# A hybrid encoder layer as one stream of matmuls: weight loads on GpSimd's queue, and three more output units in the seven-product form

## The chip, the core and the metric

The kernel runs on one core of a Trainium2 chip. A core has five engines that run side by side, each with an instruction queue of its own that is worked off strictly in order: TensorE (PE in the profile; PEld is its loading of weights), VectorE (DVE), ScalarE (ACT), GpSimd (POOL) and SyncE (SP). PE multiplies into PSUM banks; DVE and ACT read those banks and work on tiles in SBUF; SP and POOL issue the DMAs that move tiles between SBUF and DRAM. An instruction waits in its queue for semaphores of others, and all that stand behind it wait too. The metric is the device time of one execution in microseconds (us), the median of three runs.

## The reference

One layer of a streaming encoder for 1024 positions of width 1024, in float32, cut to what matters here:

```python
h = rms_norm(x, norm1_w)
q, k, v, g_ret, x_lru, y_lru, gate_ret, gate_lru = split(h @ w_in)
o = head_group_norm(chunkwise_retention(rotary(q), rotary(k), v), ret_gn_w)   # 4 heads
y_a = (o * silu(g_ret)) @ w_ret_o
hl = rg_lru(causal_depthwise_conv(x_lru))                                     # 4 blocks
y_b = (hl * gelu(y_lru)) @ w_lru_o
x = x + (sigmoid(gate_ret + b0) * y_a + sigmoid(gate_lru + b1) * y_b) @ w_out
h = rms_norm(x, norm2_w)
gate, val = split(h @ ffn_w_up)                                               # 3072 each
x = x + (gelu(causal_depthwise_conv(gate)) * val) @ ffn_w_down
return rms_norm(x, norm_f_w)
```

## The kernel before

**Products in two parts.** Each float32 operand is split into a high part in the PE's reduced float32 type and a low part, the rest (`split`: a cast on ACT, L167, and a subtraction on DVE, L168). A product of two operands takes three matmuls (`PASSES`: high x high, high x low, low x high).

**Jobs.** The large projections are cut into jobs (`Job`). A job is one unit of 256 output columns, with operand blocks B11, B12, B21, B22 (the activations: first index the half of the inner dimension, second the half of the positions) and weight blocks A11 to A22. There are 28 jobs for the input projection, 4 for the retention output (`w_ro`, operand `og`), 4 for the LRU output (`w_lo`, operand `u`), then the output projection written out by hand (L1182), 24 jobs for the up projection and 12 for the down projection.

- The *standard form* (`mm_std`, matmuls at L330) takes 8 block products of 12 matmuls, 96 in all.
- The *seven-product form* (`mm_fast`, matmuls at L387; `fast=True`) is a Strassen-like scheme with 7 block products, 84 matmuls. It needs sums of weight blocks (S1 to S4, DVE at L246, L249, L255, L262), sums of operand blocks (T1 to T4, one set for all jobs of the operand; made by `tsets` for later operands) and more evictions from PSUM (ACT copies at L402, DVE additions at L413).

`FAST_RO` and `FAST_LO` say how many of the four jobs of each output projection take the seven-product form: 0 and 3. The order of the input jobs is the string `SEQ`: `g` a merge-gate job, `y` and `x` the two LRU jobs of a block, `h` the three jobs of a retention head.

**Queues in the program.** `loads()` brings raw weight blocks from DRAM, in the order of the jobs and at most `AHEAD` = 6 ahead, with `SY.dma_start` at L208; `preps()` splits and sums them (up to `NBLK` = 7 ready). `builders` make the operand of the coming projection while the current one runs; `back` holds generators of work that follows a job (a head's retention, an LRU block, rotary tables), which are advanced a little after each product. Operands, temporaries and results share 81 buffers `u` of 128x512; weights share 22 buffers `w`. The order on each engine is chosen by the framework's scheduler from the program's order and from priorities (`hp()`).

**What is kept in DRAM between stages.** `ret_out` writes the gated retention output of each head to `og_d` (L964); a `builder` started by `og_start`, after the last input job but one, reads it back (L997) and splits it into the 32 tiles of `og`. The LRU blocks write `u_d` (L853), and `u_start`, after the third retention output job, first drains all `back` work and then starts the builder of `u`, which also makes its T sums from `u_d` (L544 to L552). LRU gate matmuls are at L814. The up projection's results go through `post_ff` (conv, gelu, product at L1219) to `ff_d` by a DMA of GpSimd (L1220); the down projection reads `ff_d` as its weight blocks (L208) and `w_dn` (L1230) as its operand, and accumulates through `x1_d` (L1260, L1274). The rotary tables use eight more DMAs of GpSimd (L741 to L744). Every other DMA is issued by SP.

Of the kernel before, what the change touches and what calls it, by code (L numbers as in the profile page):

```python
# [11 lines left out]
F32 = mybir.dt.float32  # L12
# [5 lines left out]
P = 128  # L18
D = 1024
T = 1024  # L20
KT = 8
TH = 512
# [64 lines left out]
class Units:  # L87
# [11 lines left out]
    def get(self, dt=F32):  # L99
        i = self.q.popleft()  # L100
        self.count += 1
        t = self.pool.tile(self.shape, dt, tag=f"{self.name}{i}", name=f"{self.name}{i}_{self.count}")
        self.at[id(t)] = (i, t)
        return t

    def put(self, *tiles):
        for t in tiles:
            self.q.append(self.at.pop(id(t))[0])
# [8 lines left out]
RATE = 1.0  # L117
BRATE = 3.0
RESERVE = 20
FAST_RO = 0  # L120
RO_T = 9
FAST_LO = 3
GQ = False
SEQ = "g g y0 g y1 h0 h1 h2 h3 x0 g g x1 g y2 g x2 g y3 x3"
STD_L = 2


# [1 line left out]
def tile_trunk_layer(ctx, tc, x, xt, positions, params, consts, normf, w_in, w_ro, w_lo,  # L129
                     w_out, w_up, w_dn, w_gate, out):  # L130
    nc = tc.nc
    V, S, G, PE, SY = nc.vector, nc.scalar, nc.gpsimd, nc.tensor, nc.sync
    ST = G if GQ else SY

    pool = ctx.enter_context(tc.tile_pool(name="sb", bufs=1))
    pps = ctx.enter_context(tc.tile_pool(name="ps", bufs=1, space=bass.MemoryType.PSUM))
    pdr = ctx.enter_context(tc.tile_pool(name="dr", bufs=1, space=bass.MemoryType.DRAM))
# [6 lines left out]
    get, put = U.get, U.put  # L144
# [3 lines left out]
    ident = cst[:, C_ID:C_ID + P]  # L148

    og_d = pdr.tile([KT, P, T], F32, tag="og", name="og_d")  # L150
    u_d = pdr.tile([KT, P, T], F32, tag="u", name="u_d")
    y_d = pdr.tile([KT, P, T], F32, tag="y", name="y_d")
    sg_d = pdr.tile([2, KT, P, T], F32, tag="sg", name="sg_d")
# [10 lines left out]
    def split(src, get=get):  # L164

        hi, lo = get(F32R), get(F32R)
        S.copy(hi, src)  # L167
        V.tensor_sub(lo, src, hi.bitcast(F32))  # L168
        return hi, lo
# [29 lines left out]
    def loads():  # L199
        i = 0  # L200
        while True:
            while i >= len(queue):
                yield None
            jb = queue[i]
            for nm in jb.order:
                t = W.get()
                m, kh = int(nm[1]) - 1, int(nm[2]) - 1
                SY.dma_start(t, jb.src(m, kh))  # L208
                jb.raw[nm] = t
                state["raws"] += 1  # L210
                yield True
            i += 1
# [69 lines left out]
    builders = deque()  # L282
# [29 lines left out]
    def drain():  # L312
        while back:
            advance(1e9)
# [156 lines left out]
    def pair_src(w, i):  # L471
        return lambda m, kh: w[i, 2 * m + kh]
# [58 lines left out]
    def reads(fetch, keys, ahead):  # L531

        keys, got = deque(keys), deque()
        while keys or got:
            while keys and len(got) <= ahead:
                got.append(fetch(*keys.popleft()))
            yield got.popleft()

    def tsets(op, fetch, ahead=2):
        tiles = reads(fetch, [(n, j) for j in range(4) for n in ("B11", "B12", "B21", "B22")], ahead)  # L540
        for j in range(4):
            b11, b12, b21, b22 = (next(tiles) for _ in range(4))
            t1, t2 = get(), get()
            V.tensor_sub(t1, b12, b11)  # L544
            op["T1", j] = split(t1)
            yield 1.2
            V.tensor_sub(t2, b22, t1)
            op["T2", j] = split(t2)
            yield 1.2
            V.tensor_sub(b12, b12, b22)  # L550
            op["T3", j] = split(b12)
            V.tensor_sub(t2, b21, t2)  # L552
            op["T4", j] = split(t2)
            put(t1, t2, b11, b12, b21, b22)
            yield 2.4
# [11 lines left out]
    h1, keep = {}, {}  # L567
# [324 lines left out]
    def retention_head(hd, qk, vv):  # L892
        cur = 0
        mask = cst[:, C_MASK + 128 * hd:C_MASK + 128 * hd + 128]
        for h in range(2):
# [55 lines left out]
                yield 0.3  # L951
            put(kd[h], vt[h, 0], vt[h, 1], qk[0, h], qk[1, h])

    def ret_out(hd, gg):
        for h in range(2):
            for m in range(2):
                ps = psa.get()
                for b in range(4):
                    c0 = 256 * (b % 2) + 128 * m
                    PE.transpose(ps[:, 128 * b:128 * b + 128], ob[h, b // 2][:, c0:c0 + 128], ident)  # L960
                g = gg[m, h]
                V.scalar_tensor_tensor(g, ps, pc("ret_gn_w", 2 * hd + m), g, ALU.mult, ALU.mult)
                psa.put(ps)
                ST.dma_start(og_d[2 * hd + m, :, TH * h:TH * h + TH], g)  # L964
                put(g)
                yield 0.8
            put(ob[h, 0], ob[h, 1])
        if hd == HEADS - 1:
            put(*rot.values())
# [13 lines left out]
    def operand(op, fetch, sums=True):  # L983

        keys = [(n, j) for n in ("B11", "B21", "B12", "B22") for j in range(4)]
        for key, t in zip(keys, reads(fetch, keys, 3)):
            op[key] = split(t)
            put(t)
            yield 0.6
        if sums:  # L990
            yield from tsets(op, fetch)

    def from_dram(src):
        def fetch(n, j):
            t = get()
            h = int(n[2]) - 1
            SY.dma_start(t, src[4 * (int(n[1]) - 1) + j, :, TH * h:TH * h + TH])  # L997
            return t
        return fetch
# [18 lines left out]
    def emit_ret_o(n):  # L1018
        def emit(m, h, ps, unit):
            ch = 2 * n + m  # L1020
            t = ojobs[n].take(m, h)
            V.tensor_mul(t, ps, t)
            ST.dma_start(t1_d[ch, :, TH * h:TH * h + TH], t)
            put(t)
            if unit is not None:
                put(unit)
        return emit
# [48 lines left out]
    jobs[-1].last = True  # L1076
    def og_start(post=jobs[-2].post):
        builders.append(operand(og, from_dram(og_d), False))
        return post() if post else None

    jobs[-2].post = og_start

    def og_sums():
        drain()
        if FAST_RO:
            builders.append(tsets(og, from_dram(og_d)))

    def u_start():
        drain()
# [1 line left out]

    ojobs = []
    for n in range(4):
        ojobs.append(Job(pair_src(w_ro, n), og, emit_ret_o(n), {2: u_start, RO_T: og_sums}.get(n),
                        fast=n >= 4 - FAST_RO, last=n == 3, drop12=n == 3 - FAST_RO, fetch=from_sg(0, n)))
    for n in range(4):
        ojobs.append(Job(pair_src(w_lo, n), u, emit_lru_o(n), fast=n >= 4 - FAST_LO, last=n == 3,
# [109 lines left out]
    def post_ff(i):  # L1207
        g, kh, kk = i // 8, (i % 8) // 4, i % 4
        for h in range(2):
            c = get()  # L1210
            src = gv[0, h]
            S.activation(c, src, AF.Identity, bias=pc("ffn_conv_b", i), scale=pc("ffn_conv_w", 48 + i))  # L1212
            for s in (1, 2):
                w = pc("ffn_conv_w", 24 * (2 - s) + i)
                V.scalar_tensor_tensor(c[:, s:], src[:, :TH - s], w, c[:, s:], ALU.mult, ALU.add)  # L1215
                if h == 1:
                    V.scalar_tensor_tensor(c[:, :s], gv[0, 0][:, TH - s:], w, c[:, :s], ALU.mult, ALU.add)
            S.activation(c, c, AF.Gelu_apprx_tanh)
            V.tensor_mul(c, c, gv[1, h])  # L1219
            G.dma_start(ff_d[g, 4 * h:4 * h + 4, kh, :, kk, :].rearrange("t p c -> p t c"),  # L1220
                         c.rearrange("p (t c) -> p t c", t=4))
            put(c)
        for t in gv.values():
            put(t)
# [154 lines left out]
```

## Time and profile before

| | us |
|---|---|
| median of 3 runs | 1678.83 |
| lowest and highest run | 1673.21, 1679.45 |
| profiled execution, its own time | 1675.42 |
| its span, first to last instruction | 1673.6 |

| engine | busy us | share of the span |
|---|---|---|
| PE | 1627.2 | 97% |
| PEld | 1332.6 | 80% |
| DVE | 1289.9 | 77% |
| ACT | 886.4 | 53% |
| POOL | 40.7 | 2% |

A group's row of the profile reads: line, engine, operation, output <- inputs, shapes, count | busy us, mean ns of one | idle time of the engine before them, and what ended most of it. A row of the timeline reads: start, length, engine, line, operation, count, and in brackets the idle time before it and what ended it. "SPq" and "POOLq" are the queues in which DMAs are issued. A row of waits reads: engine and line <- what it waited for: us in total, times, longest.

### The profile page before, as it was taken

The page shows a single profiled execution, that of the slowest core. Times are in us where ns is not written, and L with a number is a line of the kernel's source. Part 1 is how long each engine was busy: PE and PEld are TensorE (multiplying, and loading weights), DVE is VectorE, ACT ScalarE, POOL GpSimd, SP SyncE. Part 2 cuts the span into 40 slices and gives each one's busy share as a digit, 9 for nine tenths or more (in the row PEclk, how much of TensorE's full clock was granted, in tenths as well). Part 3 has the DMA queues.
Part 4 walks back from the last instruction along what each step waited for, and adds up shares of the span by engine and source line. Part 5 has one row for each costly group of instructions (what it writes and reads, how often), then busy time and mean ns, then how long its engine had stood idle before and what let it go on. Part 6 is the DMA issues. An engine that isn't in the chain of part 4 may idle for free.

```text
span 1673.6 us, 21183 instructions
## 1 busy us (share of the span) xinstructions
PE 1627.2 (97%) x7224; PEld 1332.6 (80%) x7224; DVE 1289.9 (77%) x2366; ACT 886.4 (53%) x1480; POOL 40.7 (2%) x60
## 2 busy tenths in 40 slices
PE   8999999999999999999999999999999999999997
PEld 6888788888888877887778788888888887777776
DVE  8998768666888889857862796777767777878886
ACT  7654444535678877753530564444444455444554
POOL 0001000000000000000000000000000000000000
PEclk9999999999999999999999999999999999999999
DMA  7243212131333348656463022222222237687851
GB/s 293 89 154 97 86 54 89 51 95 45 113 114 105 122 140 267 210 166 232 154 209 107 32 95 82 82 82 82 89 82 82 92 122 229 224 260 243 260 193 76
DMA packets 120524, 225.97 MB, mean 135 GB/s; under 512 B 14048, under 2 KB 14176, under 8 KB 120416
## 3 DMA queue, kind: packets, MB, share of 16 engines
q1 hardware_dynamic: 116192, 210.99, 39.1%
q0 software_dynamic: 4224, 13.64, 2.1%
q8 instruction: 56, 0.92, 0.2%
q14 instruction: 52, 0.43, 0.1%
HBM read 164.80 MB, written 54.53 MB: 131 GB/s over the span
## 4 chain that ended last, share of the span: by engine, by line
PE 50%; DVE 8%; DMA 6%; ACT 3%; issue 2%; SPq 0%; DVEq 0%; ACTq 0%
PE g L387 36%; PE g L330 7%; PE g L1182 4%; DMA u<-w_dn 2%; DVE u L168 2%; PE a L814 2%; DVE w L168 1%; DMA w<-ff_d 1%; DMA x_d<-u 1%; DVE u L797 1%; ACT u L167 1%; DVE u L413 1%; DMA u<-u_d 1%; PE a L513 0%; DMA u<-w_out 0%
## 5 line engine op out<-in xcount | busy, mean ns | idle before, releaser
L387 PE MATMUL g<-u,w 128*128 128x512 f32 x5124 | 1204.7, 393 | 20.1 <-ACT u L402 9.7
L387 PEld LDWEIGHTS g<-u,w 128*128 128x128 f32 x5124 | 958.9, 188 | 224.6 <-ACT u L402 14.8
L167 ACT CAST w<-w 128x512 fp32r<-128x512 f32 x471 | 291.3, 621 | 359.7 <-PE g L387 280.6
L168 DVE TENSOR_TENSOR w<-w,w 128x512 fp32r<-128x512 f32 x471 | 322.6, 686 | 90.0 <-ACT w L167 85.4
L330 PE MATMUL g<-u,w 128*128 128x512 f32 x960 | 227.2, 394 | 2.8 <-ACT u L167 2.8
L167 ACT CAST u<-u 128x512 fp32r<-128x512 f32 x232 | 139.3, 620 | 150.1 <-DVE u L552 16.1
L330 PEld LDWEIGHTS g<-u,w 128*128 128x128 f32 x960 | 181.3, 190 | 41.9 <-ACT u L167 3.2
L168 DVE TENSOR_TENSOR u<-u,u 128x512 fp32r<-128x512 f32 x232 | 154.5, 687 | 38.8 <-ACT u L167 25.9
L413 DVE TENSOR_TENSOR u<-g,u 128x512 f32<-128x512 f32 x183 | 125.6, 686 | 57.0 <-PE g L387 43.5
L402 ACT COPY u<-g 128x512 f32<-128x512 f32 x183 | 106.4, 582 | 73.8 <-PE g L387 73.7
L1182 PE MATMUL g<-u,u 128*128 128x512 f32 x384 | 90.1, 392 | 2.5 <-ACT u L167 1.6
L1182 PEld LDWEIGHTS g<-u,u 128*128 128x128 f32 x384 | 71.3, 188 | 18.4 <-ACT u L167 2.0
L1215 DVE SCALAR_TENSOR_TENSOR u<-u,par,u 128x511 f32<-128x511 f32 (+1 forms) x96 | 71.6, 747 | 6.2 <-ACT u L1212 5.5
L1220 POOL DMA_DIRECT2D ff_d<-u x48 | 36.2, 753 | 1271.0 <-DVE u L1219 1271.0
L246 DVE TENSOR_TENSOR w<-w,w 128x512 f32<-128x512 f32 x61 | 42.1, 690 | 20.6 <-DMA w<-w_up 12.6
L814 PE MATMUL a<-u,u 128*128 128x512 f32 x192 | 48.8, 394 | 4.3 <-ACT u L167 3.5
L1184 DVE TENSOR_TENSOR u<-g,u 128x512 f32<-128x512 f32 x16 | 11.1, 691 | 49.3 <-PE g L1182 49.3
L1212 ACT ACTIVATE u<-u,par 128x512 f32<-128x512 f32 x48 | 39.1, 817 | 15.7 <-DVE u L413 15.7
L814 PEld LDWEIGHTS a<-u,u 128*128 128x128 f32 x192 | 35.5, 188 | 14.3 <-ACT u L167 5.6
L249 DVE TENSOR_TENSOR w<-w,w 128x512 f32<-128x512 f32 x61 | 42.0, 688 | 0.9
L262 DVE TENSOR_TENSOR w<-w,w 128x512 f32<-128x512 f32 x61 | 41.9, 686 | 0.4
L255 DVE TENSOR_TENSOR w<-w,w 128x512 f32<-128x512 f32 x61 | 41.8, 685 | 0.3
(173 smaller groups left out, 1151.2 us busy)
## 6 DMA issues: line engine op xcount, KB each, us to landing
w<-w_in SPq DMA_DIRECT2D x112, 256.0 KB, 2.7
w<-w_up SPq DMA_DIRECT2D x96, 256.0 KB, 2.6
u<-w_dn SPq DMA_DIRECT2D x96, 256.0 KB, 4.0
u<-x_d SPq DMA_DIRECT2D x56, 256.0 KB, 5.3
x_d<-u SPq DMA_DIRECT2D x48, 256.0 KB, 3.3
ff_d<-u POOLq DMA_DIRECT2D x48, 256.0 KB, 2.5
w<-ff_d SPq DMA_DIRECT2D x48, 256.0 KB, 3.8
u<-x SPq DMA_DIRECT2D x32, 256.0 KB, 5.3
```

The source lines that it names most:

```text
L167: S.copy(hi, src)
L168: V.tensor_sub(lo, src, hi.bitcast(F32))
L246: V.tensor_add(s1, a21, a22)
L249: V.tensor_sub(s1, s1, a11)
L262: V.tensor_sub(s1, a12, s1)
L330: PE.matmul(ps[h], w[a][:, c], o[b], start=n == 0, stop=n == 23)
L387: PE.matmul(bank, w[a][:, c], need(op, (bn, j))[b], start=first and n == 0, stop=n == 11, skip_group_check=True)
L402: S.copy(u, bank)
L413: V.tensor_add(u, bank, u)
L814: PE.matmul(ps, wg[g][a][:, cs], xs[k][b], start=q == 0, stop=q == 5)
L1182: PE.matmul(ps, o[a][:, 128 * t:128 * t + 128], wo[k][b], start=n == 0, stop=n == 23)
L1215: V.scalar_tensor_tensor(c[:, s:], src[:, :TH - s], w, c[:, s:], ALU.mult, ALU.add)
```

## The change

- **Weight loads.** The raw weight blocks of all jobs but the first two are loaded by GpSimd's queue (`WQ`) instead of SP's. The stores to `ff_d` go from GpSimd's queue to SP's.
- **Retention output.** `FAST_RO` is 3: the jobs 1 to 3 take the seven-product form, job 0 the standard form. The T sums of this operand are made at heads 2 and 3: as soon as a tile of channel j + 4 is ready in `ret_out`, `out_sums` loads the two tiles of channel j (heads 0 and 1) from `og_d`, makes the four sums with four DVE subtractions and stores them to a new DRAM tile `to_d`. `kept_sums`, a second builder that `og_start` appends, reads the 16 tiles back and splits them. `og_sums` with `RO_T` and the switch `GQ` are gone.
- **Order of jobs.** `SEQ` changes: the gate between y0 and y1 and one of the two after x0 move towards the end, the y and x jobs stand one or two places earlier, and x3 is third from the end instead of last, with two gates behind it.

```diff
-FAST_RO = 0
-RO_T = 9
+FAST_RO = 3
 FAST_LO = 3
-GQ = False
-SEQ = "g g y0 g y1 h0 h1 h2 h3 x0 g g x1 g y2 g x2 g y3 x3"
+SEQ = "g g y0 y1 h0 h1 h2 h3 x0 y2 g x1 y3 g x2 g g x3 g g"
...
-    ST = G if GQ else SY
+    ST, WQ = SY, G
...
+    to_d = pdr.tile([4, 4, P, TH], F32, tag="to", name="to_d")
...
-                SY.dma_start(t, jb.src(m, kh))
+                (SY if i < 2 else WQ).dma_start(t, jb.src(m, kh))
...
+    def out_sums(j, b21, b22):
+
+        b11, b12 = get(), get()
+        for h, b in ((0, b11), (1, b12)):
+            SY.dma_start(b, og_d[j, :, TH * h:TH * h + TH])
+        yield 1.0
+        V.tensor_sub(b11, b12, b11)
+        ST.dma_start(to_d[0, j], b11)
+        yield 0.6
+        V.tensor_sub(b12, b12, b22)
+        ST.dma_start(to_d[2, j], b12)
+        put(b12)
+        yield 0.6
+        V.tensor_sub(b11, b22, b11)
+        ST.dma_start(to_d[1, j], b11)
+        put(b22)
+        yield 0.6
+        V.tensor_sub(b21, b21, b11)
+        ST.dma_start(to_d[3, j], b21)
+        put(b21, b11)
+        yield 0.6
...
     def ret_out(hd, gg):
...
                 ST.dma_start(og_d[2 * hd + m, :, TH * h:TH * h + TH], g)
-                put(g)
                 yield 0.8
+                if hd < 2:
+                    put(g)
+                elif h == 1:
+                    yield from out_sums(2 * hd - 4 + m, gg[m, 0], g)
...
+    def kept_sums(op, src):
+
+        def fetch(n, j):
+            t = get()
+            SY.dma_start(t, src[int(n[1]) - 1, j])
+            return t
+
+        keys = [(f"T{i}", j) for i in (1, 2, 3, 4) for j in range(4)]
+        for key, t in zip(keys, reads(fetch, keys, 3)):
+            op[key] = split(t)
+            put(t)
+            yield 0.6
...
         builders.append(operand(og, from_dram(og_d), False))
+        builders.append(kept_sums(og, to_d))
         return post() if post else None
...
-    def og_sums():
-        drain()
-        if FAST_RO:
-            builders.append(tsets(og, from_dram(og_d)))
...
-        ojobs.append(Job(pair_src(w_ro, n), og, emit_ret_o(n), {2: u_start, RO_T: og_sums}.get(n),
+        ojobs.append(Job(pair_src(w_ro, n), og, emit_ret_o(n), {2: u_start}.get(n),
                         fast=n >= 4 - FAST_RO, last=n == 3, drop12=n == 3 - FAST_RO, fetch=from_sg(0, n)))
...
-            G.dma_start(ff_d[g, 4 * h:4 * h + 4, kh, :, kk, :].rearrange("t p c -> p t c"),
+            ST.dma_start(ff_d[g, 4 * h:4 * h + 4, kh, :, kk, :].rearrange("t p c -> p t c"),
                          c.rearrange("p (t c) -> p t c", t=4))
```

## The prediction

> **What bounds the kernel now.** I read the page first (span, busy times, groups), then the waits of PE (TensorE), then windows of the stages that the change touches, then single stretches of the timeline and the SP queue's own waits.
>
> ```profile
> span 1673.6 us, 21183 instructions
> PE 1627.2 (97%) x7224; PEld 1332.6 (80%) x7224; DVE 1289.9 (77%) x2366; ACT 886.4 (53%) x1480; POOL 40.7 (2%) x60
> L387 PE MATMUL g<-u,w 128*128 128x512 f32 x5124 | 1204.7, 393 | 20.1 <-ACT u L402 9.7
> 352.00 17.97 PE L387 MATMUL g<-u,w 128*128 128x512 f32 x78
> 369.80 0.60 PE L885 MATMUL a<-cst,u 128*128 128x128 f32 x4
> ```
>
> PE works or holds a matmul for 97% of the span, so this kernel is a stream of matmuls with 46.4 us of holes (1673.6 - 1627.2). The 393 ns of one matmul is its latency. Its price is the distance: 78 matmuls took from 352.00 to 369.80, so 17.8 / 78 = 0.228 us each. The change can save time in two ways only: fewer matmuls, or smaller holes. It can lose time by new holes.
>
> ```profile
> 150.00:425.00 275.00, 273.07 (x1309) 225.79 (x1309) 193.04 (x428) 129.35 (x232) 0.00 (x0) 1.00 0.24 69
> 590.00:650.00 60.00, 57.86 (x251) 46.46 (x250) 53.06 (x89) 45.23 (x70) 0.00 (x0) 1.00 0.60 193
> 650.00:770.00 120.00, 115.33 (x506) 94.54 (x504) 87.20 (x146) 72.43 (x99) 0.00 (x0) 1.00 0.65 213
> 900.00:1330.00 430.00, 429.44 (x1920) 353.77 (x1920) 309.83 (x531) 204.69 (x345) 28.63 (x38) 1.00 0.25 81
> 1390.00:1600.00 210.00, 195.64 (x837) 159.02 (x836) 172.21 (x282) 99.50 (x175) 2.27 (x3) 0.98 0.74 241
> ```
>
> These windows give length, then busy time of PE, PEld, DVE (VectorE), ACT (ScalarE) and POOL (GpSimd), then clock, DMA share and GB/s. In the heads (150 to 425) and the up projection (900 to 1330) PE has 1.9 and 0.6 us of holes: nothing to win there. At the passage from input projection to the two output projections (590 to 770) the holes are 2.1 + 4.7 us, and in the passage to the down projection and inside it (1390 to 1600) they are 14.4 us.
>
> **The change, part by part.**
>
> *Three units in the seven-product form.* A standard unit is 96 matmuls, a seven-product unit 7 x 12 = 84. Three units: 36 x 0.228 = **-8.2 us**, the whole of it on the path, since PE has no other work to put there. The price is DVE and ACT work. The instruction order of the two programs gives the counts: DVE 25 more splits (L168), 12 more weight sums (L246 to L262), 9 more evictions (L413) and 16 subtractions in `out_sums`; ACT 25 more casts, 9 more copies and 14 fewer table loads.
>
> ```profile
> 1406.23 2.49 DVE L168 TENSOR_TENSOR u<-u,u 128x512 fp32r<-128x512 f32 x4
> L831 ACT ACT_TABLE_LOAD x16 | 20.5, 1283 | 0.3
> ```
>
> Four DVE instructions back to back took 2.49 us, one alone 0.69 (L413 row below), so one costs (2.49 - 0.69) / 3 = 0.60 us in a stream. DVE gets 62 x 0.60 = 37 us more. Of this, the 16 of `out_sums` (9.6 us) fall among the heads, where DVE stood idle for 82 us of 275; with their 8 loads and 16 stores on SP they cost nothing. If that cover were gone they would cost at most the 9.6 us. ACT's table loads (14 x 1.28 = 18 us less) about pay for its 34 new operations; ACT is 53% busy, so I take zero.
>
> The other 46 DVE operations (28 us) fall into 590 to 770, where DVE idles 6.9 + 32.8 us. In sum there is room; at the passage itself there is little. Here is how PE waits there now:
>
> ```profile
> 641.40 3.04 PE L387 MATMUL g<-u,w 128*128 128x512 f32 x12 [0.72 <-ACT u L402]
> 646.23 5.76 PE L387 MATMUL g<-u,w 128*128 128x512 f32 x24 [0.66 <-ACT u L402]
> 656.26 0.73 PE L814 MATMUL a<-u,u 128*128 128x512 f32 x2 [1.55 <-ACT u L167]
> 660.07 0.73 PE L814 MATMUL a<-u,u 128*128 128x512 f32 x2 [0.34 <-ACT u L167]
> 769.68 1.52 PE L330 MATMUL g<-u,w 128*128 128x512 f32 x2 [2.78 <-ACT u L167]
> ```
>
> Four holes of 3.3 us together stand at the passage. To see what comes, I count in the instruction order from the last LRU gate matmul (L814) that waits for fresh DVE work to the first retention output matmuls. Before: 40 DVE instructions to the first operand piece, against 156 matmuls; 40 x 0.60 = 24 us against 36 us: DVE is in time. After, the x3 block stands two jobs earlier and its L814 come close ahead of the passage: 44 DVE instructions to the fourth piece against 89 matmuls, 26.4 against 20.3 us, and 54 against 115 some lines on. So DVE is 6 us late by the count, and 9 with its own gaps (53.06 of 60 us busy, a tenth of 26); the two L814 rows, which end in waits, show that DVE has no lead to give when the count begins. I take 7 us of holes instead of 3.3: **+4 us**; bounds -2 (holes shrink, as the scheduler's order is only an order) and +12 (the 32 operand tiles of B and the 32 of T need 64 of 81 `u` buffers, so loads may wait for the x3 block's buffers).
>
> *The order of jobs.* x3 two jobs earlier means that the LRU work ends before the second output projection builds its operand. The 2.78 us at 769.68, where PE waits for the last `u_d` pieces, should go: **-2 us** (bounds 0 and -2.8; 0 if the buffers that the retention's T tiles hold delay the loads instead).
>
> *Weight loads to POOL, ff stores to SP.*
>
> ```profile
> SPq L208 <- PE g L387: 389.5, 98, 11.4
> SPq L208 <- DVE w L255: 221.9, 51, 6.9
> 1390.04 8.50 SPq L1230 DMA_DIRECT2D u<-w_dn  x9
> 1398.58 1.63 SPq L208 DMA_DIRECT2D w<-ff_d  x3
> 1434.35 0.88 SPq L208 DMA_DIRECT2D w<-ff_d  x2
> 1438.33 0.69 DVE L246 TENSOR_TENSOR w<-w,w 128x512 f32<-128x512 f32 x1 [1.93 <-DMA w<-ff_d]
> 1405.62 0.69 DVE L413 TENSOR_TENSOR u<-g,u 128x512 f32<-128x512 f32 x1
> PE g L387 <- ACT u L402: 6.5, 3, 4.0
> PE g L387 <- DVE u L413: 4.0, 2, 2.3
> PE g L387 <- ACT u L1218: 3.7, 1, 3.7
> ```
>
> The first two rows are waits of the SP queue at a weight load: it stands until a buffer is free, and every load and store behind it stands too. In most stages that hurts nobody (PE's holes above). In the down projection it can: nine operand loads occupy the queue for 8.5 us at 1390, and the weight loads follow behind them; at 1438.33 DVE waits 1.93 us for a weight load of 1434.35, and the 3.71 us hole of PE at 1440 ends a chain through DVE and ACT right after. The last three rows are PE's waits between 1390 and 1610, 14.2 us. On two queues a weight load goes out as soon as its buffer is free. I take a third of the 14.2: **-4.5 us**; bounds 0 and -10. DMA share there is 0.74, so the bytes themselves stay.
>
> [...]
>
> What does POOL cost?
>
> ```profile
> L1220 POOLq EVENT_SEMAPHORE  x48: 17/17/17, 135.2 to 1437.0; - x48
> L1220 POOL DMA_DIRECT2D ff_d<-u x48: 752/752/774, 977.9 to 1442.6; - x48
> 131.77 0.66 POOL L744 DMA_DIRECT2D u<-u  x1 [131.32 <-ACT u L735]
> w<-w_in SPq DMA_DIRECT2D x112, 256.0 KB, 2.7
> ff_d<-u POOLq DMA_DIRECT2D x48, 256.0 KB, 2.5
> u<-u SPq DMA_DIRECT2D x32, 128.0 KB, 2.9
> u<-u POOLq DMA_DIRECT2D x8, 128.0 KB, 3.4
> ```
>
> 280 loads move (the first two jobs' eight stay on SP). At 0.66 to 0.75 us each POOL is busy for 185 to 210 us of 1670: no bound. They land 0.2 us sooner to 0.5 us later (last two pairs of rows); blocks are loaded six ahead, so zero, bounds 0 and +3. The three comes from one place: eight rotary copies (L741 to L744) now stand on POOL with three weight loads between them and the next ones behind, and wait for ACT's sine and DVE. The 48 ff stores wait on SP for DVE (L1219), with nothing but `w_dn` and `x1_d` loads behind; those had weight loads ahead of them before. Zero.
>
> **Sum.** -8.2 + 4 - 2 - 4.5 = -10.7. The profiled execution took 1675.42 us (span 1673.6 and 1.8 around it), 3.4 below the median of the runs shown, 1678.83, and within their 1673.21 to 1679.45. 1675.4 - 10.7 = 1664.7: forecast **1665 us**.
>
> **The rivals.** (a) *The passage eats the gain.* Buffers bind: operand loads come one by one, holes of 15 instead of 3.3, and the down projection keeps its holes: -8.2 + 12 - 2 = +2, 1677. For it: DVE's 54 instructions against 115 matmuls. Against: only one passage of four gets more work. 0.22.
>
> [...] 0.14.
>
> (c) *Slower: weight blocks come late through POOL.* A load on POOL waits in order for its buffer, and the next one behind it; if issue or landing grows past the lead of the blocks, each of the 64 seven-product jobs loses a little at its first weight sum. DVE waits there already:
>
> ```profile
> DVE w L246 <- DMA w<-w_up: 12.6, 20, 2.6
> ```
>
> 20 waits of 0.63 us on average, hidden today. It decides when a load comes some 5 us later than now; at 0.4 us lost in each of 64 jobs it is +26, with the gains left 1675.4 - 10.7 + 26 = 1691. Against: 48 stores on POOL were issued in 752 to 774 ns each, while DVE was 72% busy. [...] 0.12.
>
> (d) *More:* most of the 14.2 us goes: -8.2 + 2 - 2.8 - 11 = -20, 1655. 0.08.
>
> **How the numbers follow.** The forecast (1658 to 1670) has 0.44. What a measurement of this kernel can tell from no change is about 0.5%, 8.4 us: faster means under 1670.4, slower over 1687.2. Faster: 0.44 + 0.08 + half of (b) 0.07 = 0.59, less 0.01 for the spread of runs: 0.58. Slower: (c) 0.12 and the far end of (a) 0.04 = 0.16. The rest, 0.26, is no change. Range: low end 1652, case (d) with 3 us of run spread; high end 1684, case (a) with +3 for the rotary copies and the 3.4 us by which the median stood over the profile. Above it lie (c) and the far end of (a), 0.16, and below 1652 a few hundredths.
>
> **What would show it.** Right: L330 falls from 960 to 672 matmuls and L387 rises to 5376; PE's busy time falls by about 8; PE's holes from 1380 to 1590 come to about 10 us; the wait of 2.78 at the first standard unit of the second output projection is gone; holes of some 7 us stand where retention output begins, ended by ACT or DVE at an operand split. Wrong: weight sums (L246) that wait for DMA far more than 20 times, or holes spread over all jobs (case c); holes over 12 us at the passage (a); unchanged holes in the down projection (b).

## The result and the profile after

The changed kernel takes **1702.47 us** (median; 1697.52 to 1707.49) against 1677.72 (1673.21 to 1679.45) of the kernel before beside it: ratio **1.0141, 95% interval 1.0105 to 1.0177**. It is slower by 24 us where I forecast 11 us faster, and lies above the range (1652 to 1684). The profiled execution took 1707.49 us, 5.0 above its median; the one of before (1675.42) was 2.3 below the median beside it. So the two spans differ by 32.1 us, and some 7 of them are the choice of runs.

In the changed kernel the line numbers of these stages are one smaller (L387 is now L386, L208 L207, L402 L401), and the output projection is at L1216. From the page:

```profile
span 1705.7 us, 21411 instructions
PE 1635.3 (96%) x7188; PEld 1329.5 (78%) x7188; DVE 1323.1 (78%) x2428; ACT 883.8 (52%) x1500; POOL 155.8 (9%) x292
L386 PE MATMUL g<-u,w 128*128 128x512 f32 x5376 | 1274.8, 395 | 33.8 <-ACT u L401 25.7
L329 PE MATMUL g<-u,w 128*128 128x512 f32 x672 | 163.1, 398 | 8.5 <-DVE u L167 5.8
...
L207 POOL DMA_DIRECT2D w<-w_up x96 | 51.7, 538 | 508.0 <-PE g L386 197.3
```

The 36 matmuls are gone (7188), but PE's holes grew from 46.4 to 70.4 us, and its busy time *rose* by 8.1 where it should fall by 8.2. The second sign is the granted clock: its mean over the span is 0.987 against 0.994, and 0.007 x 1706 is 12 us, an upper bound, since some of the slow time lies in the holes themselves. The windows say where, in the columns of the prediction (the last two start 20 to 25 us later than there, as the stages do):

```profile
150.00:425.00 275.00, 271.03 (x1295) 221.76 (x1296) 202.24 (x447) 124.24 (x225) 23.25 (x43) 1.00 0.30 90
590.00:650.00 60.00, 58.13 (x252) 46.52 (x251) 52.85 (x94) 40.56 (x63) 6.46 (x12) 1.00 0.46 146
650.00:770.00 120.00, 106.75 (x425) 83.62 (x423) 99.90 (x166) 78.59 (x125) 9.89 (x18) 0.91 0.68 220
770.00:880.00 110.00, 97.67 (x411) 77.76 (x409) 93.05 (x152) 51.71 (x92) 8.06 (x15) 0.97 0.68 223
920.00:1350.00 430.00, 429.44 (x1920) 353.62 (x1919) 307.00 (x529) 200.84 (x339) 42.26 (x79) 1.00 0.27 81
1415.00:1625.00 210.00, 192.99 (x815) 155.87 (x814) 167.92 (x275) 95.51 (x168) 20.43 (x38) 0.97 0.75 238
```

The window from 770 to 880 of the kernel before:

```profile
770.00:880.00 110.00, 105.22 (x442) 83.87 (x442) 87.52 (x143) 48.78 (x86) 0.00 (x0) 0.97 0.56 182
```

From 650 to 770 PE issues 425 matmuls where it had 506, at a clock of 0.91, and from 770 to 880 411 where it had 442. The up projection is untouched (0.6 us of holes), with all its weight blocks on POOL. The down projection has 17.0 us of holes for 14.4. The passage on PE, and last the start of the output projection in the kernel before:

```profile
664.55 0.79 PE L329 MATMUL g<-u,w 128*128 128x512 f32 x1 [4.94 <-DVE u L167]
717.45 0.73 PE L813 MATMUL a<-u,u 128*128 128x512 f32 x2 [1.79 <-ACT u L166]
753.91 16.41 PE L386 MATMUL g<-u,w 128*128 128x512 f32 x60 [4.21 <-ACT u L401]
811.40 0.80 PE L386 MATMUL g<-u,w 128*128 128x512 f32 x1 [3.65 <-ACT u L166]
866.17 5.74 PE L386 MATMUL g<-u,w 128*128 128x512 f32 x24 [2.78 <-ACT u L401]
871.75 5.15 PE L1216 MATMUL g<-u,u 128*128 128x512 f32 x22
...
846.89 1.43 PE L1182 MATMUL g<-u,u 128*128 128x512 f32 x5 [1.60 <-ACT u L167]
```

The output projection starts at 871.75; before it was 846.89. That is 24.9 us lost before it, with 8.2 us less to do. The other 7.2 of the 32.1 us come after it, 5.8 of them from the down projection on. Most holes end at ACT: a cast of an operand (L166), or the copy that empties a PSUM bank (L401) standing in ACT's queue behind such a cast. ACT ahead of 753.91:

```profile
752.76 0.62 ACT L166 CAST u<-u 128x512 fp32r<-128x512 f32 x1 [6.59 <-DMA u<-u_d]
753.28 0.58 ACT L401 COPY u<-g 128x512 f32<-128x512 f32 x1
```

The cast waited 6.59 us for a load of `u_d`, and the copy on which PE depends waited behind it. After the hole at 753.91 sixty matmuls take 16.4 us, and at 0.228 us each they should take 13.7, or 13.9 to the end of the last: this hole costs 2.5 us more than its own length.

The waits that my rival (c) named are there as well:

```profile
DVE w L245 <- DMA w<-w_up: 22.1, 20, 1.6
DVE w L245 <- DMA w<-ff_d: 9.8, 5, 3.2
DVE w L245 <- DMA w<-w_in: 6.3, 9, 1.8
PE g L386 <- ACT u L401: 25.7, 14, 4.4
```

### The profile page after: what moved, and what is told of

Same layout as the page of the kernel before. It is cut to its first block, busy times and chain, and to the rows that moved or that the text cites. A ratio compares the mean times of both kernels' runs of the same rounds, so it can differ in the third digit from the quotient of the medians.

```text
span 1705.7 us, 21411 instructions
## 1 busy us (share of the span) xinstructions
PE 1635.3 (96%) x7188; PEld 1329.5 (78%) x7188; DVE 1323.1 (78%) x2428; ACT 883.8 (52%) x1500; POOL 155.8 (9%) x292
## 4 chain that ended last, share of the span: by engine, by line
PE 40%; DMA 4%; issue 3%; DVE 2%; ACT 1%; SPq 0%; POOL 0%; DVEq 0%; ACTq 0%; POOLq 0%
PE g L386 33%; PE g L1216 4%; PE g L329 2%; DMA u<-w_dn 1%; DMA u<-w_out 1%; DMA w<-ff_d 1%; DMA u<-x_d 1%; PE a L512 0%; DVE u L167 0%; ACT u L166 0%; DVE w L167 0%; DMA ff_d<-u 0%; DVE u L1322 0%; ACT u L401 0%; ACT u L1335 0%
## 5 line engine op out<-in xcount | busy, mean ns | idle before, releaser
L386 PE MATMUL g<-u,w 128*128 128x512 f32 x5376 | 1274.8, 395 | 33.8 <-ACT u L401 25.7
L386 PEld LDWEIGHTS g<-u,w 128*128 128x128 f32 x5376 | 1010.7, 189 | 252.0 <-ACT u L401 33.0
L166 ACT CAST w<-w 128x512 fp32r<-128x512 f32 x480 | 295.8, 621 | 365.7 <-PE g L386 275.0
L167 DVE TENSOR_TENSOR w<-w,w 128x512 fp32r<-128x512 f32 x480 | 328.1, 685 | 80.1 <-ACT w L166 77.8
L166 ACT CAST u<-u 128x512 fp32r<-128x512 f32 x248 | 149.3, 620 | 182.5 <-DVE u L551 23.7
L167 DVE TENSOR_TENSOR u<-u,u 128x512 fp32r<-128x512 f32 x248 | 165.6, 687 | 42.4 <-ACT u L166 32.9
L412 DVE TENSOR_TENSOR u<-g,u 128x512 f32<-128x512 f32 x192 | 131.7, 686 | 55.6 <-PE g L386 37.5
L401 ACT COPY u<-g 128x512 f32<-128x512 f32 x192 | 111.7, 582 | 74.1 <-PE g L386 66.7
L207 POOL DMA_DIRECT2D w<-w_in x104 | 56.6, 544 | 551.8 <-PE g L386 265.1
L207 POOL DMA_DIRECT2D w<-w_up x96 | 51.7, 538 | 508.0 <-PE g L386 197.3
L1216 PE MATMUL g<-u,u 128*128 128x512 f32 x384 | 89.7, 392 | 2.5 <-ACT u L166 2.5
L1216 PEld LDWEIGHTS g<-u,u 128*128 128x128 f32 x384 | 71.5, 188 | 17.6 <-ACT u L166 2.9
L1249 DVE SCALAR_TENSOR_TENSOR u<-u,par,u 128x511 f32<-128x511 f32 x96 | 71.7, 747 | 6.1 <-ACT u L1246 5.4
L245 DVE TENSOR_TENSOR w<-w,w 128x512 f32<-128x512 f32 x64 | 44.2, 690 | 40.0 <-DMA w<-w_up 22.1
L1218 DVE TENSOR_TENSOR u<-g,u 128x512 f32<-128x512 f32 x16 | 11.0, 691 | 48.3 <-PE g L1216 48.2
L207 POOL DMA_DIRECT2D w<-ff_d x48 | 25.8, 538 | 244.8 <-PE g L329 100.4
L248 DVE TENSOR_TENSOR w<-w,w 128x512 f32<-128x512 f32 x64 | 43.9, 686 | 0.8
```

What stands on the lines that cost most here:

```text
L207: (SY if i < 2 else WQ).dma_start(t, jb.src(m, kh))
L245: V.tensor_add(s1, a21, a22)
L248: V.tensor_sub(s1, s1, a11)
L386: PE.matmul(bank, w[a][:, c], need(op, (bn, j))[b], start=first and n == 0, stop=n == 11, skip_group_check=True)
L401: S.copy(u, bank)
L412: V.tensor_add(u, bank, u)
```

## The experiments

Three theories to begin with. **P:** the passage loses it, through the seven-product jobs and the new order. **Q:** the queue move loses it. **S:** the order of jobs does. All distances in this table are (ratio to executions of the kernel before, taken beside the run, - 1) x 1675 us, with their 95% intervals. Runs are compared by these distances; a median belongs to its own group of executions.

| run | what | us against before |
|---|---|---|
| changed kernel | all three edits | +23.6 (17.6 to 29.6) |
| e1 | queue move alone | +10.6 (7.2 to 13.9) |
| e2 | order of jobs alone | +0.5 (-1.8 to 2.8) |
| e3 | seven-product jobs alone | +20.9 (17.9 to 24.0) |
| e4 | seven-product jobs and order | +11.7 (8.4 to 15.2) |
| e5 | e1, old order on PE, DVE, ACT | +13.1 (9.5 to 16.4) |
| e6 | before, with e1's order on PE, DVE, ACT | +41.9 (39.4 to 44.4) |
| e7 | changed, e4's order on PE, DVE, ACT | +27.0 (21.9 to 32.2) |
| e8 | e4, 16 subtractions on GpSimd | +18.3 (15.6 to 20.8) |
| e9 | e1, 24 weight buffers | +16.8 (12.1 to 21.4) |
| e10 | before, 24 weight buffers | -2.7 (-6.0 to 0.7) |
| e11 | e4 without T tiles | +4.5 (1.5 to 7.4) |
| e12 | e4, low parts by ACT | +9.9 (6.7 to 13.1) |
| e13 | e5, old order on SP and POOL too | +2.3 (0.3 to 4.4) |
| e14 | e13, rotary copies on SP | +4.9 (2.5 to 7.4) |
| e15 | e4, reserve of 8 buffers | +16.4 (12.1 to 20.8) |
| e16 | e4 with one seven-product job | +2.7 (0.0 to 5.4) |
| e17 | changed, e4's order on all engines | +20.4 (16.8 to 24.1) |
| e18 | e11 with the 32 buffers held | +8.9 (5.7 to 12.1) |

### Which edit

**e1 to e4**, by these lines of the diff, alone or together:

```diff
 # e1 and e2: no seven-product jobs, no out_sums, no kept_sums
-FAST_RO = 3
+FAST_RO = 0
 # e1 and e3: the old order of jobs
-SEQ = "g g y0 y1 h0 h1 h2 h3 x0 y2 g x1 y3 g x2 g g x3 g g"
+SEQ = "g g y0 g y1 h0 h1 h2 h3 x0 g g x1 g y2 g x2 g y3 x3"
 # e2, e3 and e4: weight loads on SyncE, ff stores on GpSimd
-    ST, WQ = SY, G
+    ST, WQ = SY, SY
```

> Only the queue move: weight loads of all jobs but the first two on GpSimd's queue, ff stores on SyncE's; order of jobs and retention output as before. Theory P (the loss is made at the passage to the output projections, by the three seven-product jobs and the new order): 1670 to 1682, within 0.4% of before. Theory Q (the loss is made by the queue move, since operand loads and weight loads no longer share one order): 1692 to 1702, most of the +24.7. Theory S (the loss is made by the new order of jobs): 1670 to 1682.

> Only the new order of the input jobs. Theory S: 1690 to 1702. Theories P and Q: within 6 us of before, 1672 to 1684; my prediction had -2.

> Only the three seven-product retention output jobs with their sums made at the heads and kept in DRAM; old order, old queues. Theory P: 36 matmuls less (-8.2) and the passage's new holes and its slower clock (about +33 in the changed kernel), so 1690 to 1702. Theories Q and S: the gain comes through, 1668 to 1674.

> The changed kernel with its queues put back (weight loads on SyncE, ff stores on GpSimd): seven-product jobs and new order stay. Theory P: 1692 to 1704, the loss stays. Theory Q: 1664 to 1674. Theory S: 1690 to 1704.

Medians 1684.99, 1675.29, 1695.58 and 1686.47. No single theory holds: the queue move costs some 10 us, the seven-product jobs 21, the order nothing by itself. Beside the seven-product jobs the order is worth 9 us (e3 to e4), which is the step "x3 earlier" that I had at 2. In e3, with the old order, its trace is 2.4 us behind before where the retention output ends and 23.7 where the LRU output ends. With 36 matmuls less it should be 8.2 ahead by then, so some 10.6 us are lost up to the first place and 21.3 in the LRU output projection. PE waits there for casts and for DVE (timeline of e3, PE; the first row is of the start of the retention output):

```profile
650.98 7.34 PE L386 MATMUL g<-u,w 128*128 128x512 f32 x24 [3.21 <-ACT u L401]
779.60 0.80 PE L329 MATMUL g<-u,w 128*128 128x512 f32 x1 [5.94 <-ACT u L166]
816.56 23.77 PE L386 MATMUL g<-u,w 128*128 128x512 f32 x91 [5.46 <-DVE u L1070]
```

### Why the queue move costs

The move changes more than a queue: the scheduler made another order on every engine. In e1 275 of 2350 DVE, 126 of 1372 ACT and 76 of the 542 SP instructions common to both stand elsewhere than before. **e5, e6, e7** separate order from queue by ordering edges that add no semaphore (in outline):

```diff
     with tile.TileContext(nc) as tc:
         tile_trunk_layer(tc, **args, out=y)
+        hold_order(tc)   # for a, b in zip(row, row[1:]) of PE, DVE, ACT:
+                         #     tc.add_manual_dep(b, a.name, NoSync)
```

> The kernel of e1 (only the queue move), with the order of the instructions on PE, DVE and ACT held to that of the kernel before by ordering edges; only the queue of the weight loads and of the ff stores differs from before. The scheduler had given e1 another order: 275 of 2350 DVE, 126 of 1372 ACT and 109 of 7102 PE instructions stand elsewhere. Theory O (the queue move costs through the order that the scheduler makes of it): back to 1672 to 1679. Theory T (the queue move costs by its transfers or by DVE and GpSimd in each other's way): 1683 to 1688, as e1 (1684.99).

> The mirror of e5: the queues of before (weight loads on SyncE, ff stores on GpSimd), with the order on PE, DVE and ACT held to that of e1. Theory O: the loss comes without the queue move, 1682 to 1690. Theory T: 1672 to 1679.

> The changed kernel with its new queues, and the order on PE, DVE and ACT held to that of e4 (the changed kernel on the old queues). Theory O: near e4, 1684 to 1690. Theory T: 1698 to 1707, as the changed kernel (1702.47).

1685.65 and 1703.44: with the old order on PE, DVE and ACT the loss stays, so theory O falls. That DVE and GpSimd get in each other's way, one of the two causes in theory T, no run here shows. The places differ, though. Of the 9.3 us by which e1's trace ends behind that of before, 4.0 are lost in the second job, where PE has a hole of 2.16 us at 44.86; e5's trace loses nothing there, and as much in sum elsewhere. e6 (1715.95) is no mirror image. e1's order has the splits of weight blocks early; on SyncE those blocks go out from 27.13 us on, behind 16 loads of x rows, and what stands behind the splits waits, already in the first job (timeline of e6, SyncE and PE):

```profile
16.56 10.19 SPq L563 DMA_DIRECT2D u<-x  x16
27.13 29.05 SPq L208 DMA_DIRECT2D w<-w_in  x6
...
33.57 11.59 PE L363 MATMUL g<-u,w 128*128 128x512 f32 x36 [10.36 <-ACT u L580]
```

An order fits only the queues it was made for.

**e9, e10** test rival (c), that weight blocks come late:

```diff
-NU = 81
-NW = 22
-AHEAD = 6
+NU = 79
+NW = 24
+AHEAD = 8
```

> e1 (only the queue move) with more lead for the weight blocks: 24 instead of 22 weight buffers and 8 instead of 6 blocks loaded ahead, paid with 2 of the 81 u buffers. To be read against e10, the kernel before with the same buffers. Theory L (on GpSimd's queue each weight block lands about 0.5 us later after its buffer comes free, and DVE's first weight sum waits for it; the lead is bound by buffers): the distance to e10 shrinks from 9.8 to 0 to 4 us. Theory I (the loss is not in the lead of the blocks: rotary copies and other work on the moved queues): the distance stays at 8 to 11 us.

> The kernel before with 24 weight buffers, 8 blocks ahead and 79 u buffers: the control of e9. Both theories: within 6 us of before (1669 to 1681); if L holds, rather below it, as DVE's first weight sums wait 20.6 us for loads in the kernel before too.

1694.05 against 1673.36: the distance did not shrink, it grew from 10.6 to 19.5 us. Yet the suspected wait was gone. Groups of the first weight sum in e9 (idle time and its cause last):

```profile
L245 DVE TENSOR_TENSOR w<-w,w 128x512 f32<-128x512 f32 x61 | 41.9, 687 | 2.1 <-PE g L386 1.2
```

So taking DVE's wait for weight blocks away does not bring the time back. But e9 is not e1 without the wait: it has an order of its own, and 8.0 of the 17.6 us between the traces of e9 and e10 are lost in the second job, where e9 has a hole of 6.81 us at 47.82. That the wait is not what the move costs rests on the next runs, which keep it.

**e13, e14** hold SyncE and GpSimd to the old order as well, and e14 puts the rotary copies on SyncE (in outline):

```diff
-        # e5: PE, DVE, ACT
+        # e13: all five, in the order of the kernel before
-            G.dma_start(c[0:64, :], f[src, :])   # e14: all eight copies
+            SY.dma_start(c[0:64, :], f[src, :])
```

> e5 (queue move alone, order on PE, DVE and ACT as before) with the instructions of SyncE and GpSimd also held to the order in which they stood in the kernel before; only the queue of each weight load and ff store differs from before. Theory SP (the loss at the LRU output comes from another order of SyncE's other loads): 1676 to 1681, with the 3.9 us of the rotary copies left. Theory T (GpSimd's queue itself is slower): 1683 to 1688, as e5 (1685.65).

> e13 with the eight rotary copies issued by SyncE instead of GpSimd. Theory R (three of the copies stand behind a weight load that waits for its buffer, and the first head waits for them): 3 to 4 us less than e13; with theory SP too, 1673 to 1678. If the copies are not it: as e13.

1678.51: **of e5's 13.1 us 2.3 are left.** So most of that loss is the order on these two queues. 39 of SyncE's 542 common instructions stood elsewhere in e5, and on GpSimd's queue one weight load and one rotary copy had changed places; the run does not part the two. Theory SP has the time right, but not the place. At the LRU output, SyncE in e5:

```profile
779.00 0.32 SPq L1031 DMA_DIRECT2D u<-u_d  x1
781.57 4.49 SPq L1048 DMA_DIRECT2D u<-t_d  x3
786.10 1.01 SPq L1041 DMA_DIRECT2D u<-sg_d  x2
788.09 0.32 SPq L1031 DMA_DIRECT2D u<-u_d  x1
```

and in e13:

```profile
777.61 0.32 SPq L1031 DMA_DIRECT2D u<-u_d  x1
780.13 3.84 SPq L1048 DMA_DIRECT2D u<-t_d  x2
784.10 0.36 SPq L1041 DMA_DIRECT2D u<-sg_d  x1
786.03 0.32 SPq L1031 DMA_DIRECT2D u<-u_d  x1
```

Between two operand loads of `u_d` stand three `t_d` and two `sg_d` loads in e5, two and one in e13 and in the kernel before, and `u_d` goes out 2 us later. But this costs nothing: by the starts of the same matmuls, PE in e5 is 2.4 us behind e13 at 769 us already, and 1.9 at 800. Of the 5.8 us by which e5's trace ends behind that of e13, 2.5 are lost at the first head, 1.5 around the start of the output projection and 2.3 in the down projection, where most of the moved SyncE instructions stand (loads of `w_dn` and `x1_d`). At the first head the changed place is that of the rotary copy (PE in e5, then in e13):

```profile
152.10 1.09 PE L884 MATMUL a<-cst,u 128*128 128x128 f32 x4 [2.12 <-DVE u L877]
...
151.85 0.66 PE L884 MATMUL a<-cst,u 128*128 128x128 f32 x4 [1.21 <-DVE u L877]
```

In e13 the first weight sums wait for loads as long as in the changed kernel, and twice as long as before; with it the whole move costs 2.3 us (groups of e13, then of before):

```profile
L245 DVE TENSOR_TENSOR w<-w,w 128x512 f32<-128x512 f32 x61 | 42.2, 691 | 40.6 <-DMA w<-w_up 22.5 <-DMA w<-w_in 10.6 <-DMA w<-ff_d 6.9
```

```profile
L246 DVE TENSOR_TENSOR w<-w,w 128x512 f32<-128x512 f32 x61 | 42.1, 690 | 20.6 <-DMA w<-w_up 12.6 <-DMA w<-ff_d 4.1 <-DMA w<-w_in 3.6
```

e14 (1679.91) gave nothing. On SyncE the copies stand between other copies of the first head and the last goes out at 139.54 us, later than on POOL in e13 (138.19; before 135.62), so theory R is neither shown nor excluded. PE waits 1.70 us at the first head there too.

**e17** does to the changed kernel what e13 did to e1:

> The changed kernel with the instructions of all five engines held to the order in which they stand in e4 (the changed kernel on the old queues, 1686.47): only the queue of each weight load and ff store differs from e4. Theory SP (the queue move costs by the order of SyncE's other instructions, which the scheduler chose anew): 1686 to 1692, 10 us or more under the changed kernel. Theory T (the queue of GpSimd is slower by itself): 1696 to 1706, near e7 (1703.44).

1695.39, between the two. Against e4 the queue move is worth 12 us in the changed kernel (15 in e7), and 9 with all orders held. Here the order of SyncE would explain 3 to 7 us, and the intervals overlap, so that even this is not settled. The other 9 us stay open. By the same matmuls e17's trace is 4.8 us behind e4's at 842 us, gathered from 150 us on in steps of 1 to 2.5 us, and 9.7 at 880. The start of the output projection lies between (PE in e17, then in e4):

```profile
869.80 15.38 PE L1216 MATMUL g<-u,u 128*128 128x512 f32 x57 [4.49 <-ACT u L166]
...
861.75 8.70 PE L1216 MATMUL g<-u,u 128*128 128x512 f32 x37 [2.84 <-ACT u L166]
```

### What the seven-product jobs lose

DVE's load in the passage, e2 (without the jobs) and e4 (with them), same order of jobs:

```profile
650.00:770.00 120.00, 113.99 (x497) 92.64 (x496) 87.23 (x143) 60.95 (x96) 0.00 (x0) 1.00 0.75 246
770.00:880.00 110.00, 105.04 (x452) 85.23 (x452) 88.37 (x143) 47.99 (x85) 0.00 (x0) 0.98 0.54 176
```

```profile
650.00:770.00 120.00, 108.81 (x448) 85.89 (x447) 104.71 (x175) 77.52 (x127) 0.00 (x0) 0.96 0.72 231
770.00:880.00 110.00, 102.66 (x433) 81.17 (x432) 96.80 (x159) 51.80 (x90) 0.00 (x0) 0.98 0.69 226
```

DVE rises from 175.6 to 201.5 us of 230, near the 28 that I counted, and stands idle for 12% of the time. **e8 and e12** take 16 operations from it in two ways, **e11** leaves the T tiles (the split sums of operand blocks) out. The code is cut to the lines that matter:

```diff
-            op[key] = split(t)                      # kept_sums
+            G.tensor_sub(lo, t, hi.bitcast(F32))    # e8: low part on GpSimd
+            S.copy(lo, t)                           # e12: low part on ACT
+        op[f"T{i}", j] = op["B11", j]               # e11: no T tiles
```

> e4 (seven-product jobs and new order on the old queues, 1686.47) with the 16 subtractions that split the kept T sums moved from DVE to GpSimd, which is idle there; nothing else moves. Theory D (DVE work sets the pace between the input projection and the output projection): 16 x 0.6 = 9.6 us of DVE time come off the path, 1674 to 1681. Theory B (u buffers and the loads behind them set the pace): within 3 us of e4, 1683 to 1690.

> e4 with the low parts of the 16 T tiles written by a second copy on ACT instead of the subtraction on DVE: the low part is then the rounded value itself, the subtraction is left out. DVE loses 16 operations of 0.6 us, ACT gets 16 of 0.58 us, buffers and loads stay. Theory D with DVE as the limit: 1676 to 1681. Theory B (buffers and loads): 1683 to 1690. If ACT is what is late: 1687 to 1695.

> e4 (seven-product jobs and new order on the old queues, 1686.47) without the tiles of the T sums: the 16 loads from DRAM, 16 casts on ACT, 16 subtractions on DVE and 32 buffers are left out, and the matmuls read the tiles of B11 in their place; the 36 fewer matmuls, the weight sums and the evictions stay. Theory D (DVE and ACT work of the T tiles late at the passage): 1666 to 1674, the gain of 8.2 comes through. Theory E (the weight sums and evictions of three more seven-product jobs, 30 more DVE operations of 0.6 us, set the pace): 1679 to 1686.

e8 was slower (1692.02): one subtraction takes 1533 ns on GpSimd against 0.69 us on DVE, and PE has one hole of 8.07 us at 714 (group and timeline row of e8):

```profile
L1028 POOL TENSOR_TENSOR u<-u,u 128x512 fp32r<-128x512 f32 x16 | 24.4, 1533 | 576.1 <-PE g L386 541.3 <-ACT u L1027 16.6 <-issue 11.3
```

```profile
714.48 4.45 PE L386 MATMUL g<-u,w 128*128 128x512 f32 x12 [8.07 <-ACT u L401]
```

e12 (1687.34) is not to be told from e4: moving 9.6 us from DVE to ACT wins nothing that these runs can tell. So DVE's sum of work alone is not the limit. e11 (1679.47) wins 7 us. The intervals of e4 and e11 do not meet.

**e15, e18** ask whether that is the lateness of the T tiles, their buffers, or their work. Counted in the program, fewer than 20 `u` buffers are free at 12 of 16 steps of the first two retention output jobs in e4 (9 to 26; before 27 to 37), and 20 is the reserve below which builders rest.

```diff
+        state["reserve"] = 8                                    # e15
+        op[f"T{i}", j] = op["B11", j] + (get(F32R), get(F32R))  # e18
```

> e4 (seven-product jobs and new order on the old queues, 1686.47) with the builders of the retention operand allowed to run until 8 instead of 20 u buffers are free, up to the start of the LRU operand. In e4 fewer than 20 are free at nearly every step of the first two retention output jobs, so that T tiles are made on demand, just ahead of the matmul that reads them. Theory B (this lateness is the 7 us that e11 won): 1678 to 1683. Rival (the buffers are then missing elsewhere, or the lateness is hidden): 1685 to 1692.

> e11 (e4 without the T tiles, 1679.47) with their 32 u buffers taken and given back as in e4, but without loads, casts and subtractions: the matmuls read B11 in their place, as in e11. Theory B (the buffers are what the T tiles cost): 1684 to 1690, as e4. Theory W (their loads, casts and subtractions are): 1677 to 1682, as e11.

e15 (1693.72) is 4.7 us above e4, with intervals that just overlap: earlier T tiles win nothing, so theory B in that form falls; that they take buffers from others would fit. e18 (1683.53) lies between e11 and e4, 4.4 above the first and 2.8 below the second, and its interval overlaps both: it points to the buffers for more than half of the 7 us, and does not settle it. It does hold the buffers as e4 does (10 to 27 free at the same 16 steps), and its trace points the same way: between 600 and 842 us e11 gains 6.0 us on e4, and e18 1.4.

**e16** keeps all T tiles and makes one job of the three a seven-product job (`FAST_RO = 1`):

> e4 with one seven-product job instead of three (FAST_RO = 1): 24 matmuls more (+5.5), 20 DVE operations fewer (12 us), the sums and all T tiles stay. Theory E (the DVE work of the seven-product jobs sets the pace there): 1676 to 1682. If only the T tiles and their buffers cost: 1687 to 1693.

1679.95, 9 us better than e4 with 24 matmuls *more*. So two further jobs, in place of saving 5.5 us, cost 9: each pays some 7 us in holes and clock for 2.7 us of matmuls. T tiles and buffers alone would not do that, since e16 keeps both: 10 to 22 buffers are free in its first two jobs. That is what theory E foretold, but it is not theory E alone. e16 also needs the T tiles first in the fourth job, where e4 needs them in the second, and no run parts that from the weight sums and evictions; and e12 says that it is not DVE's time in sum. One way in which it happens is seen at 752.76 in the changed kernel: a PSUM eviction stands in ACT's queue behind a cast whose load has not come.

One hole is the same in all of these runs. e16 has it at the first matmul of the retention output:

```profile
661.50 0.80 PE L329 MATMUL g<-u,w 128*128 128x512 f32 x1 [4.80 <-DVE u L167]
```

In e4 it is 4.61 us long, in the changed kernel 4.94 (at 664.55 above), and e11, without T tiles, waits 4.31 at 660.19. In e2, with the same order of jobs, no hole there reaches 1 us. So it comes with the seven-product edit, but goes neither with the T tiles nor with two of the three jobs; its cause stays open.

No version here beats the kernel before: e2 and e10 are not to be told from it.

## Why the prediction was wrong, by its steps

**Minus 8.2 for 36 matmuls, "the whole of it on the path": the count held, the path did not.** In the passage PE did not set the end. e11 has the 36 fewer matmuls and is 4.5 us slower than before.

**"In sum there is room; at the passage there is little", +4 (bounds -2 and +12): this step failed, and by most.** With the new order the jobs cost 11.7 net, so the passage took about 20 (11.7 + 8.2), beyond the far bound. I set 28 us of DVE work against idle DVE time of 590 to 770 and looked only at where the retention output begins. The work goes on to 870, and idle time of DVE was no measure of room: in e4 DVE stands idle for 12% of that stretch while PE waits. The hole that I forecast at the first operand piece, 7 us ended by ACT or DVE, did come, with 4.94 us; but I had worked it out from x3's new place, and e2 has that place without the hole. The bound for buffers (64 of 81) was named and given 12 us together with all else; e18 puts it at some 4, without settling it. Left out altogether was the clock: 24 matmuls take 7.34 us after a hole of 3.21 in e3, and 5.76 after one of 0.66 in the prediction's row. Two windows of e3 right behind that hole (time, PE busy and matmuls, granted clock):

```profile
650.98:654.38 3.40, 3.40 (x8) 0.50 0.88 326
654.38:657.78 3.40, 3.40 (x16) 1.00 0.55 158
```

At a clock of 0.50 8 matmuls stand in the window, and at 1.00 16 in the next. The length of the hole alone does not decide. After one of 2.78 us the clock is 0.50 in the kernel before (769.68 to 773.08, right behind the hole in the prediction's row) and 1.00 in the changed kernel (866.17 to 869.57). After one of only 1.79 us, at 717.45 in the changed kernel, it is 0.50 from 719.15 to 720.85. After one of 3.40 in e1 12 matmuls take 3.02 us, no longer than the 3.04 after 0.72 in the prediction's row; the 12 behind the 8.07 us in e8 take 4.45:

```profile
1408.52 3.02 PE L386 MATMUL g<-u,w 128*128 128x512 f32 x12 [3.40 <-ACT u L401]
```

The stretch at 0.50 agrees with the loss: the 1.58 us more that the 24 matmuls of e3 took (7.34 - 5.76) are, by my estimate from these rows, 7 matmuls at double price (7 x 0.228 = 1.6), 3.2 us at half speed. What besides the hole lowers the clock, no run shows.

**x3 two jobs earlier, -2:** the 2.78 us hole at 769.68 went and others took its place; +0.5 alone. Its worth of 9 us shows only where the LRU operand is late (e3 to e4).

**Queue move, -4.5 (bounds 0 and -10), and POOL at 0 (bounds 0 and +3): sign wrong.** Alone it costs +10.6. Seen right: SyncE's queue matters. Missed: a queue that loses a third of its instructions gets a new order of the rest from the scheduler, and holding that order takes most of the loss away (e5 to e13). Which of the changed places cost it is not shown. With the order held, the move costs 2.3 us and still gains nothing: of the 14.2 us of holes in the down projection, e13's trace wins back 1.9 (its distance to before falls from 5.8 us at the up projection to 3.9 at the end). The rotary copies, named as the place of the +3, are late in e5 (three of them behind a weight load, and the first head 3.9 us late), but e14 could not show it. The ff stores, costed at zero, were not moved alone.

**The rivals.** (a) had the right place and the wrong size: its +12 at the passage was 20. (c) named its sign to watch, L245 waiting for DMA. It came (38 us for 20), and it was not the cause of what the queue move costs by itself: e13 has the same waits at +2.3, and e9 has none at +16.8. For the 9 us that e17 leaves open it is not excluded. The 48 issues on POOL, 752 to 774 ns each, were a fair reason against it: in the changed kernel 96 loads of the up projection took 538 ns each (median; the longest 547), with PE at 99.9%. (b) was right that the queue move wins nothing, not that it is free.

The changed kernel's +23.6 then stands as: queue move +10.6, seven-product jobs +20.9, order +0.5, and -8.4 because the edits act on each other, chiefly the order on the jobs (e3 to e4, 9.2).

## What to carry to other kernels

Saved matmuls count only where PE sets the end: before crediting them, look at the stage's DVE and ACT as queues, at the buffers that the extra operands hold, and add for the clock: the matmuls here took 1.6 us longer behind a PE hole of 3.21 us (e3), 2.5 behind one of 4.21 (changed kernel) and 1.4 behind one of 8.07 (e8), but no longer behind one of 3.40 (e1). Moving DMAs to another queue under a scheduler that chooses the order on each engine is two edits: hold the order of all engines, the queue's own above all, to see which one costs. A wait that doubles in the profile proves nothing until it has been taken away alone.

## What the runs showed that I had not expected

The three largest groups of weight loads, 256 KB each, land later from GpSimd's queue than from SyncE's, by 0.2 to 0.6 us: median 2.9 against 2.7 for `w_in`, 2.9 against 2.6 for `w_up`, and in e5 4.4 against 3.8 for `ff_d` (rows of before, then of e5). It is no rule for every load: the 16 of `w_ro` took 3.0 us in the changed kernel against 4.0 before.

```profile
w<-w_up SPq DMA_DIRECT2D x96, 256.0 KB, 2.6
```

```profile
w<-w_up POOLq DMA_DIRECT2D x96, 256.0 KB, 2.9
w<-ff_d POOLq DMA_DIRECT2D x48, 256.0 KB, 4.4
```

With ordering edges alone, and no operation, queue or byte changed, a kernel moved by 42 us (e6) and by 11 (e5 to e13): the order alone can weigh more than the three edits together.
